# Sums of squares of all norms by products with a column of ones instead of transposes and a reduction

## The chip, the cores and the metric

The program runs on one core of one Trainium2 chip. The metric is the device time of one execution in microseconds. Five engines work side by side, each through its own queue in order: TensorE (PE; its weight loads are listed apart as PEld), VectorE (DVE), ScalarE (ACT), GpSimd (POOL) and SyncE (SP, which issues DMAs). Matmul results land in PSUM, from which VectorE and ScalarE read.

## The reference

The model is a trunk of two layers over 512 tokens of 1024 channels, in float32. Each layer runs three token mixers side by side (differential attention with 4 heads, a convolution module with a depthwise convolution of 31 taps, and neighbourhood attention), merges them by gates, adds the result to the stream, and goes on with a SwiGLU feed-forward and a gated input embedding. Norms stand ahead of each part:

```python
def rmsnorm(x, g):
    x32 = x.astype(jnp.float32)
    y = x32 * lax.rsqrt(jnp.mean(x32 * x32, axis=-1, keepdims=True) + EPS)
    return (y * g.astype(jnp.float32)).astype(x.dtype)
...
for i in range(DEPTH):
    h = rmsnorm(x, norm_mix[i])
    ya = diff_attention(...)       # rmsnorm over 128 channels of each of 4 heads
    yb = conformer_conv(...)       # layernorm over 512 channels
    yc = neighbourhood_attention(...)
    x = x + merged @ w_o[i]
    h = rmsnorm(x, norm_ffn[i])
    x = x + (jax.nn.silu(h @ w_ffn_gate[i]) * (h @ w_ffn_up[i])) @ w_ffn_down[i]
    h = rmsnorm(x, norm_ple[i])
    x = x + jax.nn.sigmoid(h @ w_ple_gate[i]) * (p[i] @ w_ple_in[i])
return rmsnorm(x, norm_final)
```

So 17 means of squares over channels are needed: per layer 3 of the trunk, 4 of the heads and 1 of the convolution, and the final one.

## The kernel before

Activations lie transposed: 128 channels on the partitions, all 512 tokens along the free axis, eight such tiles for 1024 channels. A weight matrix comes in by 128x1024 pieces, and each is split into a high and a low float32r half (ScalarE copies the high half, L143; VectorE subtracts it, L157). A product is then three matmuls of 512 columns (high by high, high by low, low by high, L177 to L179). The feed-forward uses a scheme with 256-column matmuls (L1100).

A norm over channels is a sum across partitions. The squares are first added over the tiles into one 128x512 tile, named `ss` (`sumsq`, or one ScalarE square for a head). Then `norm`, a generator, does the rest. It yields numbers of ticks, so that its parts fall between other matmuls of the stream: TensorE's order is that in which the code issues its instructions, and a tick is four chunks of a product. After the first yield, TensorE transposes `ss` in four 128x128 blocks (L213) into one PSUM bank of the tag `tr`, which has two banks; so the tokens come to the partitions, and the channels' partial sums along the free axis. VectorE adds along that axis (L215) to 128x4 numbers, `sm`: one for each of 512 tokens. A small VectorE operation divides by the number of channels and adds epsilon (L218; for the heads L160, with an epsilon of each token's own). GpSimd raises that to the power -0.5 (L222, `rc`). After the second yield, TensorE turns these columns back into a bank that holds each token's factor on all partitions (L226), ScalarE copies it, and the waiting tiles are multiplied by it.

`main_norm` runs this for the trunk: once in the opening, and in each layer after the output projection (tile `wo_ss`) and after the feed-forward (`ffn_ss`), and once after the first layer's embedding (`ple_ss`). `conv` runs it in each layer, and `diff_unit` once for each head. That is 16 runs. The final norm has code of its own: it takes the sums of six of its eight tiles by four products with a column of ones (L1401), and the rest by VectorE.

Only TensorE's order is fixed by the code. The queues of the other engines are ordered by a scheduler, by priorities and estimated times; so a removed instruction can change the order of others. Pools rotate their buffers: `tr` over two PSUM banks, `sm` over eight small tiles. The names in rows are tiles, with the part of the model in which they were made as a prefix (`diff_tr` is a `tr` bank of the differential attention, `diff_pt` the split transposed probabilities, `pin` and `gateb` projections beside the convolution).

Of the kernel before, what the change touches and what calls it, by code (L numbers as in the profile page):

```python
# [15 lines left out]
ALU = mybir.AluOpType  # L16
AX = mybir.AxisListType
# [3 lines left out]
P = 128  # L21
# [40 lines left out]
class Net:  # L62
# [143 lines left out]
    def norm(self, sq, n, waits, done, spread=True, eps=None):  # L206


        nc = self.nc
        yield waits[0]  # L210
        st = self.ps("tr", (P, 4, P))
        for c in range(4):
            nc.tensor.transpose(st[:, c, :], sq[:, c * P:(c + 1) * P], self.ident)  # L213
        sm = self.sb("sm", [P, 4])
        nc.vector.tensor_reduce(out=sm, in_=st, op=ALU.add, axis=AX.X)  # L215
        ms = self.sb("sm", [P, 4])
        if eps is None:
            nc.vector.tensor_scalar(ms, sm, 1.0 / n, EPS, ALU.mult, ALU.add)  # L218
        else:
            self.stt(ms, sm, 1.0 / n, eps, ALU.mult, ALU.add)  # L220
        col = self.sb("rc", [P, 4])
        nc.gpsimd.tensor_tensor(col, ms, self.power, ALU.pow)  # L222
        yield waits[1]
        bc = self.ps("tr", (P, 4, P))
        for c in range(4):
            nc.tensor.transpose(bc[:, c, :], col[:, c:c + 1].to_broadcast([P, P]), self.ident)  # L226
        bc = bc.rearrange("p a b -> p (a b)")
        done(col, self.spread(bc) if spread else bc)
# [1309 lines left out]
```

## Time and profile before

| | |
|---|---|
| median of 3 runs | 1781.59 us (1780.82 to 1783.68) |
| profiled execution | 1781.65 us |
| its span, first to last instruction | 1779.9 us |
| TensorE matmuls (PE) | 1767.4 us busy, 99% of the span |
| TensorE weight loads (PEld) | 1551.4 us, 87% |
| VectorE (DVE) | 1372.7 us, 77% |
| ScalarE (ACT) | 897.9 us, 50% |
| GpSimd (POOL) | 63.5 us, 4% |
| mean DMA rate | 145 GB/s |

The profile is one execution. In its rows of groups stand line, engine, operation, the tiles (out<-in), the count, and durations in nanoseconds. In rows of the timeline stand start and duration in microseconds, and in brackets the idle time of the engine ahead of that instruction and what ended it. Matmuls are pipelined and overlap, so their durations are longer than the steps between their starts.

### The profile page before, as it was taken

Reading aid. Unit: us, or ns where it says so; the run is one execution under the profiler, and the core shown is the slowest. Engines: PE = TensorE matmul, PEld = TensorE weight load, DVE = VectorE, ACT = ScalarE, POOL = GpSimd, SP = SyncE. Lnnn points to the kernel's source line nnn. Section 1 sums busy time; section 2 is a strip of 40 time slices with the busy share of each in tenths; the row PEclk is TensorE's granted clock in tenths of the full one; section 3 lists DMA queues with packets and bytes.
Section 4 is the critical chain, followed back from the end, with each engine's and each line's share of the span. In section 5 each row is a group of like instructions: output and inputs, shape, how many; then the busy total and the mean of one; then the engine's idle time right before and its main releaser. Section 6 shows DMA issues by size and latency. Waiting matters only on the chain.

```text
span 1779.9 us, 26531 instructions
## 1 busy us (share of the span) xinstructions
PE 1767.4 (99%) x10019; PEld 1551.4 (87%) x10019; DVE 1372.7 (77%) x2113; ACT 897.9 (50%) x1480; POOL 63.5 (4%) x102
## 2 busy tenths in 40 slices
PE   9999999999999999999999999999999999999998
PEld 7888888888899899898878888888888998998987
DVE  7789787897877577577786788879878775775776
ACT  5566555425665255255545664563356652542544
POOL 0000000000010000000000000000000100100000
PEclk9999999999999999999999999999999999999999
DMA  5767443325556366253437564433363662663332
GB/s 190 190 180 189 125 130 93 104 97 163 198 157 180 131 166 189 79 141 115 159 121 189 177 181 119 133 87 107 101 199 133 196 190 84 186 181 107 116 110 95
DMA packets 98384, 257.51 MB, mean 145 GB/s; under 512 B 12880, under 2 KB 17616, under 8 KB 98256
## 3 DMA queue, kind: packets, MB, share of 16 engines
q1 hardware_dynamic: 90912, 231.00, 41.4%
q0 software_dynamic: 6336, 23.07, 7.1%
q8 instruction: 79, 1.29, 0.3%
q10 hardware_dynamic: 1008, 1.75, 0.3%
q14 instruction: 49, 0.40, 0.1%
HBM read 216.44 MB, written 7.86 MB: 126 GB/s over the span
## 4 chain that ended last, share of the span: by engine, by line
PE 96%; DVE 2%; issue 1%; DMA 0%; ACT 0%; SPq 0%; POOL 0%; POOLq 0%; DVEq 0%; ACTq 0%
PE ffn_sc L1100 14%; PE ffn_av L1100 7%; PE ffn_mm L177 4%; PE ffn_mm L178 4%; PE ffn_mm L179 4%; PE ffn_tr L1100 4%; PE mergea_mm L179 2%; PE mergea_mm L177 2%; PE mergea_mm L178 2%; PE wo_mm L178 2%; PE wo_mm L179 2%; PE wo_mm L177 2%; PE gateb_mm L178 2%; PE gateb_mm L179 2%; PE gateb_mm L177 2%; PE natten_mm L177 1%
## 5 line engine op out<-in xcount | busy, mean ns | idle before, releaser
L143 ACT ACTIVATE ffn_wh<-ffn_wr 128x1024 fp32r<-128x1024 f32 (+1 forms) x114 | 117.3, 1029 | 183.2 <-PE ffn_mm L178 102.7
L160 DVE SCALAR_TENSOR_TENSOR conv_z<-glu_z,pre_par,conv_z 128x512 f32<-128x512 f32 x240 | 179.3, 747 | 3.0
L157 DVE TENSOR_TENSOR ffn_wl<-ffn_wr,ffn_wh 128x1024 fp32r<-128x1024 f32 (+1 forms) x114 | 135.0, 1184 | 46.5 <-ACT ffn_wh L143 46.0
L1100 PE MATMUL ffn_sc<-wo_h,ffn_wh 128*128 128x256 f32 x704 | 130.4, 283 | 0.0
L1100 PEld LDWEIGHTS ffn_sc<-wo_h,ffn_wh 128*128 128x128 f32 x704 | 110.4, 192 | 0.8
L1100 PE MATMUL ffn_sc<-wo_h,ffn_wl 128*128 128x256 f32 x352 | 99.6, 283 | 0.0
L177 PE MATMUL ffn_mm<-ffn_z,ffn_wh 128*128 128x512 f32 x240 | 93.4, 389 | 0.0
L178 PE MATMUL ffn_mm<-ffn_z,ffn_wh 128*128 128x512 f32 x240 | 93.4, 389 | 0.0
L179 PE MATMUL ffn_mm<-ffn_z,ffn_wl 128*128 128x512 f32 x240 | 93.4, 389 | 0.0
L157 DVE TENSOR_TENSOR ffn_t<-ffn_mm,wo_r 128x512 f32<-128x512 f32 x48 | 33.1, 689 | 72.3 <-PE ffn_mm L179 72.3
L157 DVE TENSOR_TENSOR ffn_wl<-ffn_rp,ffn_wh 128x1024 fp32r<-128x1024 f32 x44 | 53.8, 1222 | 30.1 <-ACT ffn_wh L143 30.1
L143 ACT ACTIVATE mergea_wh<-mergea_wr 128x1024 fp32r<-128x1024 f32 (+1 forms) x32 | 27.1, 847 | 88.8 <-PE mergea_mm L178 80.4
L1100 PEld LDWEIGHTS ffn_sc<-wo_h,ffn_wl 128*128 128x128 f32 x352 | 67.5, 192 | 0.0
L1100 PE MATMUL ffn_sc<-wo_qk,ffn_wh 128*128 128x256 f32 x352 | 67.1, 283 | 0.0
L1100 PE MATMUL ffn_sc<-wo_v,ffn_wh 128*128 128x256 f32 x352 | 67.1, 283 | 0.0
L1100 PE MATMUL ffn_av<-wo_h,ffn_wh 128*128 128x256 f32 x352 | 65.3, 283 | 0.0
L143 ACT ACTIVATE ffn_wh<-ffn_rp 128x1024 fp32r<-128x1024 f32 x44 | 46.4, 1055 | 29.4 <-PE ffn_mm L178 17.5
L905 DVE TENSOR_REDUCE diff_s<-diff_sc 128x1 f32<-128x512 f32 x64 | 42.7, 685 | 16.1 <-PE diff_sc L808 15.9
L1100 PEld LDWEIGHTS ffn_sc<-wo_qk,ffn_wh 128*128 128x128 f32 x352 | 54.9, 192 | 0.0
L1100 PEld LDWEIGHTS ffn_av<-wo_h,ffn_wh 128*128 128x128 f32 x352 | 54.9, 192 | 0.0
L1100 PEld LDWEIGHTS ffn_sc<-wo_v,ffn_wh 128*128 128x128 f32 x352 | 54.9, 192 | 0.0
L179 PEld LDWEIGHTS ffn_mm<-ffn_z,ffn_wl 128*128 128x128 f32 x240 | 45.1, 188 | 9.4
(726 smaller groups left out, 5635.4 us busy)
## 6 DMA issues: line engine op xcount, KB each, us to landing
ffn_wr<-w_gu SPq DMA_DIRECT2D x66, 512.0 KB, 4.2
ffn_e<-w_gu SPq DMA_DIRECT2D x32, 512.0 KB, 3.4
ffn_e<-w_gu POOLq DMA_DIRECT2D x32, 512.0 KB, 8.0
ffn_wr<-w_fd SPq DMA_DIRECT2D x32, 512.0 KB, 4.7
natten_wr<-w_in SPq DMA_DIRECT2D x16, 512.0 KB, 4.5
natten_b<-bias SPq DMA_DIRECT2D x32, 256.0 KB, 4.3
gatec_wr<-w_in SPq DMA_DIRECT2D x16, 512.0 KB, 4.4
diff_wr<-w_in SPq DMA_DIRECT2D x16, 512.0 KB, 4.7
```

The costliest lines, as they stand in the source:

```text
L143: i = self.nc.scalar.activation(out, in_, func, **kw)
L157: return self.nc.vector.tensor_tensor(out, a, b, op)
L160: return self.nc.vector.scalar_tensor_tensor(out, a, s, b, op0, op1)
L177: mm(out, wh, ah, start=first, stop=False)
L178: mm(out, wh, al, start=False, stop=False)
L179: mm(out, wl, ah, start=False, stop=last)
L905: nc.vector.tensor_reduce(out=m[:, u:u + 1], in_=sc, op=ALU.max, axis=AX.X, negate=True)
L1100: mm(bank[:, u], w[:, u, kp], t, start=begin and n == 0, stop=False, skip_group_check=True)
```

## The change

In `norm`, the four transposes of the squares are replaced by four matmuls: the block of squares is the stationary operand, and one column of ones is the moving one. Each gives a column of 128 sums, one for each token of the block, so the sums come out of TensorE finished, as 128x4 numbers in PSUM. The VectorE reduction is gone, and the small operation reads the sums from PSUM. All 16 runs of `norm` change; the final norm does not. Both operands are float32, as in the final norm's products. From the line after the matmul on, line numbers are one lower than before.

```diff
         nc = self.nc
         yield waits[0]
-        st = self.ps("tr", (P, 4, P))
+        sm = self.ps("tr", (P, 4))
         for c in range(4):
-            nc.tensor.transpose(st[:, c, :], sq[:, c * P:(c + 1) * P], self.ident)
-        sm = self.sb("sm", [P, 4])
-        nc.vector.tensor_reduce(out=sm, in_=st, op=ALU.add, axis=AX.X)
+            nc.tensor.matmul(sm[:, c:c + 1], sq[:, c * P:(c + 1) * P], self.ones[:, 0:1],
+                             start=True, stop=True)
         ms = self.sb("sm", [P, 4])
         if eps is None:
             nc.vector.tensor_scalar(ms, sm, 1.0 / n, EPS, ALU.mult, ALU.add)
```

On TensorE the places stay the same. Around the second layer's convolution norm there stands before:

```order
L179 MATMUL pin_sc_12459<-pin_e_12357,pin_wl_12462 128x512
L213 MATMUL conv_tr_12472<-pre_ident_95,conv_ss_12395 128x128 x4
L177 MATMUL gateb_mm_12486<-ple_h_8751,gateb_wh_12488 128x512
L178 MATMUL gateb_mm_12486<-ple_h_8751,gateb_wh_12488 128x512
L179 MATMUL gateb_mm_12486<-ple_h_8751,gateb_wl_12489 128x512
```

and now:

```order
L179 MATMUL pin_sc_12433<-pin_e_12331,pin_wl_12436 128x512
L213 MATMUL conv_tr_12446<-pre_ones_102,conv_ss_12369 128x1 x4
L177 MATMUL gateb_mm_12458<-ple_h_8733,gateb_wh_12460 128x512
L178 MATMUL gateb_mm_12458<-ple_h_8733,gateb_wh_12460 128x512
L179 MATMUL gateb_mm_12458<-ple_h_8733,gateb_wl_12461 128x512
```

Only the group in the second row is another instruction; the same holds for all 16.

VectorE at that norm, before:

```order
L157 TENSOR_TENSOR pin_wl_12559<-pin_wr_12557,pin_wh_12558 128x256
L215 TENSOR_REDUCE conv_sm_12477<-conv_tr_12472 128x4
L157 TENSOR_TENSOR gateb_wl_12575<-gateb_wr_12573,gateb_wh_12574 128x1024
L218 TENSOR_SCALAR conv_sm_12479<-conv_sm_12477 128x4
L157 TENSOR_TENSOR conv_z_8801<-conv_z_8801,conv_r_12510 128x512
```

and now:

```order
L157 TENSOR_TENSOR pin_wl_12531<-pin_wr_12529,pin_wh_12530 128x256
L217 TENSOR_SCALAR conv_sm_12451<-conv_tr_12446 128x4
L157 TENSOR_TENSOR gateb_wl_12547<-gateb_wr_12545,gateb_wh_12546 128x1024
L157 TENSOR_TENSOR conv_z_8783<-conv_z_8783,conv_r_12482 128x512
L157 TENSOR_TENSOR conv_z_9753<-conv_z_9753,conv_r_12482 128x512
```

The reduction is gone, and the small operation on `conv_sm` now stands ahead of the weight split `gateb_wl` instead of behind it.

VectorE behind the norm of the first head (first layer), where the probabilities of the next head are made (`diff_s`, `diff_a`) and transposed (`diff_pt`), before:

```order
L905 TENSOR_REDUCE diff_s_2474<-diff_sc_2475 128x1
L157 TENSOR_TENSOR diff_rp_2393<-diff_rp_2393,diff_kh_2253 128x512
L905 TENSOR_REDUCE diff_s_2474<-diff_sc_2481 128x1
L160 SCALAR_TENSOR_TENSOR conv_z_1492<-glu_z_318,pre_par_67,conv_z_1492 128x512
L157 TENSOR_TENSOR diff_pt_2519<-diff_tr_2514,diff_pt_2519 128x512
L910 RECIPROCAL diff_s_2474<-diff_s_2474 128x1
L160 SCALAR_TENSOR_TENSOR conv_z_1492<-glu_z_318,pre_par_67,conv_z_1492 128x512
L160 SCALAR_TENSOR_TENSOR diff_s_2474<-diff_s_2474,natten_nlam_540,diff_sm_2000 128x1
L157 TENSOR_TENSOR diff_pt_2527<-diff_tr_2522,diff_pt_2527 128x512
L157 TENSOR_TENSOR gatec_wl_2736<-gatec_wr_2734,gatec_wh_2735 128x1024
L160 SCALAR_TENSOR_TENSOR diff_a_2479<-diff_e_2485,diff_s_2474,diff_a_2479 128x512
```

and now:

```order
L904 TENSOR_REDUCE diff_s_2470<-diff_sc_2471 128x1
L904 TENSOR_REDUCE diff_s_2470<-diff_sc_2477 128x1
L157 TENSOR_TENSOR diff_rp_2391<-diff_rp_2391,diff_kh_2251 128x512
L160 SCALAR_TENSOR_TENSOR conv_z_1490<-glu_z_316,pre_par_67,conv_z_1490 128x512
L909 RECIPROCAL diff_s_2470<-diff_s_2470 128x1
L157 TENSOR_TENSOR diff_pt_2515<-diff_tr_2510,diff_pt_2515 128x512
L160 SCALAR_TENSOR_TENSOR diff_s_2470<-diff_s_2470,natten_nlam_538,diff_sm_1998 128x1
L160 SCALAR_TENSOR_TENSOR conv_z_1490<-glu_z_316,pre_par_67,conv_z_1490 128x512
L160 SCALAR_TENSOR_TENSOR diff_a_2475<-diff_e_2481,diff_s_2470,diff_a_2475 128x512
L157 TENSOR_TENSOR gatec_wl_2732<-gatec_wr_2730,gatec_wh_2731 128x1024
L157 TENSOR_TENSOR diff_pt_2523<-diff_tr_2518,diff_pt_2523 128x512
```

The second `diff_pt` moved from ahead of `gatec_wl` and `diff_a` to behind them, and the first from ahead of the reciprocal to behind it. ScalarE's queue shows the matching move there: the second copy to `diff_pt` now stands behind the second exponential (`diff_e`). Behind the second head's norm the second `diff_pt` moves too, behind `diff_a` alone, while the first stays ahead of the reciprocal. In the second layer the moves are the same.

## The prediction

> **What bounds the kernel now.** I read the page first: busy shares, granted clock, chain of work.
>
> ```profile
> span 1779.9 us, 26531 instructions
> ...
> PE 1767.4 (99%) x10019; PEld 1551.4 (87%) x10019; DVE 1372.7 (77%) x2113; ACT 897.9 (50%) x1480; POOL 63.5 (4%) x102
> ...
> PEclk9999999999999999999999999999999999999999
> ...
> PE 96%; DVE 2%; issue 1%; DMA 0%; ACT 0%; SPq 0%; POOL 0%; POOLq 0%; DVEq 0%; ACTq 0%
> ```
>
> TensorE is busy for 99% of the span at full clock, and 96% of the chain that ended last is its own work, with VectorE at 2%. Since the ends of matmuls are modelled, I take no busy time as a price. I go by steps, from the start of one matmul to the start of the next, and by the table of what TensorE waited for:
>
> ```profile
> PE diff_av L177 <- DVE diff_v L157: 2.8, 2, 1.4
> ...
> PE ple_tr L213 <- DVE ple_ss L157: 1.0, 1, 1.0
> PE natten_mm L598 <- DVE natten_t L160: 0.8, 1, 0.8
> ...
> PE conv_tr L226 <- POOL conv_rc L222: 0.4, 1, 0.4
> ```
>
> These waits come to 5.0 us in 1780. The first three are for the split of the values, for a sum of squares not yet added, and for a projection; in none is the norm's VectorE reduction the last thing. Only the fourth lies behind a norm's sums. So what the change adds to TensorE's stream should be paid nearly in full, and what it takes from VectorE should return only where TensorE stands behind a norm.
>
> **How often.** The edited lines run once per norm. The transposes they remove, by tile:
>
> ```profile
> L213 PE MATMUL diff_tr<-pre_ident,diff_ss x32: 270/272/273, 236.9 to 1204.8; 128*128 128x128 f32 x32
> ...
> L213 PE MATMUL conv_tr<-pre_ident,conv_ss x8: 271/272/273, 414.2 to 1296.0; 128*128 128x128 f32 x8
> ...
> L213 PE MATMUL wo_tr<-pre_ident,wo_ss x8: 272/272/273, 502.5 to 1382.2; 128*128 128x128 f32 x8
> ...
> L213 PE MATMUL ffn_tr<-pre_ident,ffn_ss x8: 270/272/273, 850.0 to 1729.7; 128*128 128x128 f32 x8
> ...
> L213 PE MATMUL glu_tr<-pre_ident,glu_ss x4: 271/272/273, 27.9 to 28.2; 128*128 128x128 f32 x4
> ...
> L213 PE MATMUL ple_tr<-pre_ident,ple_ss x4: 272/272/303, 895.6 to 896.0; 128*128 128x128 f32 x4
> ```
>
> That is 64 transposes, four to a norm: 16 norms (8 of attention heads, 2 of the convolution, 6 of the trunk). The seventeenth, at the kernel's end, doesn't use this code.
>
> **Removed from TensorE: four transposes.** The timeline of TensorE around the first head's norm:
>
> ```profile
> 236.68 0.39 PE L179 MATMUL gateb_mm<-glu_h,gateb_wl 128*128 128x512 f32 x1
> 236.91 0.60 PE L213 MATMUL diff_tr<-pre_ident,diff_ss 128*128 128x128 f32 x4
> 237.26 0.48 PE L808 MATMUL diff_sc<-diff_qk 128*128 128x512 f32 x1
> 237.58 0.40 PE L808 MATMUL diff_sc<-diff_x,diff_qk 128*128 128x512 f32 x1
> ```
>
> The four start at 236.91 and the next matmul at 237.26: 0.35 us. That next one takes 0.32 us instead of the 0.23 of the step before the group; its weights could not be loaded under a long matmul. I expect this 0.09 us after the new products too, which are as short, so it drops out.
>
> **Added to TensorE: four products with one column.** This very form stands in the kernel's last stage, where the last norm gets most of its sums so:
>
> ```profile
> 1761.28 0.60 PE L1344 MATMUL ple_av<-pre_ident,ple_h 128*128 128x128 f32 x4
> 1761.63 0.36 PE L1337 MATMUL ple_mm<-ple_wh,ffn_v 128*128 128x256 f32 x1
> ...
> 1762.31 0.28 PE L1339 MATMUL ple_mm<-ple_wh,ffn_v 128*128 128x256 f32 x1
> 1762.43 0.95 PE L1401 MATMUL ple_mm<-pre_ones,ple_ss 128*128 128x1 f32 x8
> 1763.24 0.41 PE L1344 MATMUL ple_tr<-pre_ident,ple_h 128*128 128x128 f32 x2
> ```
>
> ```profile
> L1401 PE MATMUL ple_mm<-pre_ones,ple_ss x8: 166/250/250, 1762.4 to 1763.1; 128*128 128x1 f32 x8
> ```
>
> Four products in the code are eight matmuls in the trace: a product of two float32 operands goes through the array twice, each pass with its own load of 128x128 weights, while a transpose goes once. From 1762.43 to the next start at 1763.24 it is 0.81 us; four transposes nearby take 1761.63 - 1761.28 = 0.35 us, as above. One column instead of 128 saves nothing, since the pass lasts as long as its load, about 0.10 us. So a norm costs 0.81 - 0.35 = 0.46 us more on TensorE, and 16 norms 7.4 us. Its lower end is 0, if the second pass vanished under the neighbours; its upper end is 0.46 + 0.09 = 0.55 us a norm (8.8 in all), if the load after the group were less covered than now. I take 0.46: same form, same operands' types.
>
> [...]
>
> **Removed from VectorE: the sum along rows.**
>
> ```profile
> L215 DVE TENSOR_REDUCE diff_sm<-diff_tr x8: 682/684/686, 240.0 to 1205.9; 128x4 f32<-128x512 f32 x8
> ...
> L215 DVE TENSOR_REDUCE ffn_sm<-ffn_tr x2: 692/692/692, 850.6 to 1730.0; 128x4 f32<-128x512 f32 x2
> ...
> L1404 DVE TENSOR_SCALAR ple_sm<-ple_mm x1: 163/163/163, 1763.4 to 1763.4; 128x4 f32<-128x4 f32 x1
> ```
>
> Sixteen of 0.684 to 0.692 us are 11.0 us of VectorE. The small operation behind them now reads PSUM; L1404 does just that in 0.163 us, so it costs nothing more. VectorE is 77% busy and TensorE seldom waits for it, so I book the 11.0 us at zero, except where TensorE stands behind them. There are two such places.
>
> The first is the second layer's convolution norm:
>
> ```profile
> 1296.29 0.69 DVE L215 TENSOR_REDUCE conv_sm<-conv_tr 128x4 f32<-128x512 f32 x1 [1.10 <-PE conv_tr L213]
> 1296.90 1.22 DVE L157 TENSOR_TENSOR gateb_wl<-gateb_wr,gateb_wh 128x1024 fp32r<-128x1024 f32 x1
> 1298.03 0.16 DVE L218 TENSOR_SCALAR conv_sm<-conv_sm 128x4 f32<-128x4 f32 x1
> ```
>
> ```profile
> 1298.37 1.01 POOL L222 TENSOR_TENSOR conv_rc<-conv_sm,pre_power 128x4 f32<-128x4 f32 x1 [89.62 <-DVE conv_sm L218]
> ```
>
> ```profile
> 1298.61 0.39 PE L179 MATMUL gateb_mm<-ple_h,gateb_wl 128*128 128x512 f32 x1
> 1299.43 0.65 PE L226 MATMUL conv_tr<-pre_ident,conv_rc 128*128 128x128 f32 x4 [0.43 <-POOL conv_rc L222]
> ```
>
> From 1298.61 to 1299.43 is 0.82 us where a step is 0.23: a stall of 0.59 us. A weight split of 1.22 us stands between the reduction and the small operation; in the new order nothing does. The small operation starts 0.98 us after the products (1763.41 - 1762.43 at the end of the kernel), GpSimd's power is then done about 1.3 us before TensorE arrives, and the 0.59 us goes (at least 0, at most 0.59).
>
> The second is a transpose that waited for a PSUM bank which a reduction still read:
>
> ```profile
> PEld diff_tr L862 <- DVE diff_sm L215: 0.3, 1, 0.3
> ```
>
> The small operation frees the bank some 0.5 us sooner, and TensorE comes 0.46 us later: 0.3 us goes.
>
> **What moves.** TensorE's order stands but for the substituted group. VectorE's and ScalarE's queues change their order in both layers behind the first two head norms. ScalarE now does the second exponential ahead of the second copy of transposed probabilities, and VectorE finishes that copy's remainder (diff_pt) after a weight split and a combination of probabilities instead of before (at the second head, after the combination alone). What waits for it on TensorE is the product with the values:
>
> ```profile
> 245.33 0.69 DVE L157 TENSOR_TENSOR diff_pt<-diff_tr,diff_pt 128x512 fp32r<-128x512 f32 x1
> 245.93 1.22 DVE L157 TENSOR_TENSOR gatec_wl<-gatec_wr,gatec_wh 128x1024 fp32r<-128x1024 f32 x1
> 247.06 0.75 DVE L160 SCALAR_TENSOR_TENSOR diff_a<-diff_e,diff_s,diff_a 128x512 f32<-128x512 f32 x1
> ...
> 248.82 0.28 PE L177 MATMUL diff_av<-diff_pt,diff_v 128*128 128x256 f32 x1
> ```
>
> It ends at 246.02 and the product starts at 248.82: 2.8 us of room, against 1.22 + 0.75 = 1.97 us put ahead of it and 0.69 taken out. I book 0 at all four places. No DMA moves.
>
> **The sum.** 7.4 - 0.6 - 0.3 = +6.5 us. The profiled execution took 1781.65 us (the span and 1.75 us around it); the median of the runs is 1781.59, the same. So 1788.1 us, 0.36% slower. From no change a measurement of this kernel can tell about 0.2%, 3.6 us: the forecast lies outside.
>
> **Rivals.**
>
> Same: the extra passes vanish in TensorE's slack. The load column is busy 87% of the span, not 99%, so 228 us would be open to loads, and eight loads for four might fit under the 512-column neighbours. Then the 7.4 us goes, the 0.9 us of credits stays, and the time is 1780.8. Against it: at 1762.43 the next matmul did wait 0.81 us. [...] Chance 9%.
>
> Faster: VectorE is what really holds TensorE back, through lateness that the wait table spreads over other names. The place is the mixer stages, where diff_av and natten_mm wait. Price: 11.0 us returned against 7.4 added is -3.6, 1778.0 us. It decides only if nearly 11 us of TensorE's idle time ends, and there are 1779.9 - 1767.4 = 12.5 us of it in all; the four listed waits, 5.0 us, would leave +2.1. Chance 3%.
>
> [...] Chance 2%.
>
> Slower by a new wait: the diff_pt remainder comes late at the four places. Without its cover it could cost 1.97 us at each first head and 0.75 at each second, 5.4 more: 1793.5 us. It decides once more than 2.8 us are put ahead of it. Chance 3%.
>
> **How the numbers follow.** The forecast holds 83%. Its low end takes the two waits for diff_v (2.8 us) as gone too: 1785.3. Its high end takes the products at their upper price, 8.8, and drops both credits: 1790.4. The range 1785.2 to 1790.5 leaves out the rivals, 17%. Slower 83 + 2 + 3 = 88%, same 9%, faster 3%.
>
> **What would show it.** After: 128 short matmuls at the norms' line, each group holding TensorE for about 0.81 us; no reduction on VectorE there, its busy time down by 11; no wait of conv_tr for GpSimd. Wrong, if the groups hold TensorE for 0.4 us, or if TensorE's waits fall by more than 4 us or grow by more than 2.

## The result

The changed kernel takes 1789.75 us in the median (1788.45 to 1790.43), the kernel before 1781.59: a ratio of 1.0044, with a 95% interval of 1.0031 to 1.0057. It is slower by 8.2 us; the forecast was 6.5 us slower. The profiled execution took 1790.43 us, 1.73 us more than its span of 1788.7 us, and the span has grown by 8.8 us.

The page of the profile after, shares and chain:

```profile
span 1788.7 us, 26635 instructions
...
PE 1775.4 (99%) x10083; PEld 1559.6 (87%) x10083; DVE 1362.8 (76%) x2097; ACT 899.0 (50%) x1480; POOL 67.5 (4%) x102
...
PE 86%; DVE 2%; DMA 2%; ACT 0%; SPq 0%; issue 0%; POOLq 0%; POOL 0%; DVEq 0%; ACTq 0%
```

TensorE has 64 more instructions (10083 against 10019) and is busy 8.0 us longer. VectorE has 16 fewer and is busy 9.9 us less, and the kernel is slower all the same. The products' line of the profile after, first and last tile:

```profile
L213 PE MATMUL diff_tr<-pre_ones,diff_ss x64: 164/250/250, 238.1 to 1212.3; 128*128 128x1 f32 x64
...
L213 PE MATMUL ple_tr<-pre_ones,ple_ss x8: 242/250/250, 900.0 to 900.7; 128*128 128x1 f32 x8
```

There are 128 matmul records for 64 products, eight to a norm; a record is called a pass below. TensorE's timeline of the profile after, at the first head's norm:

```profile
237.90 0.39 PE L179 MATMUL gateb_mm<-glu_h,gateb_wl 128*128 128x512 f32 x1
238.13 0.95 PE L213 MATMUL diff_tr<-pre_ones,diff_ss 128*128 128x1 f32 x8
238.94 0.49 PE L807 MATMUL diff_sc<-diff_qk 128*128 128x512 f32 x1
239.26 0.40 PE L807 MATMUL diff_sc<-diff_x,diff_qk 128*128 128x512 f32 x1
```

The group holds the stream from 238.13 to 238.94, 0.81 us, and the matmul behind it takes 0.32 us (238.94 to 239.26), as it did behind the transposes. Over the 16 norms, from the first short matmul to the start of the next long one, the groups take 13.00 us; before they took 5.70 us. The difference is 7.3 us, 0.46 a norm. What TensorE waited for, after:

```profile
PE diff_av L177 <- DVE diff_v L157: 2.8, 2, 1.4
...
PE ple_tr L213 <- DVE ple_ss L157: 1.0, 1, 1.0
PE diff_av L597 <- DVE natten_y L157: 0.8, 1, 0.8
PE natten_mm L597 <- DVE natten_t L160: 0.8, 1, 0.8
```

The wait of conv_tr for GpSimd is gone from the list, and the wait for natten_y is new. The second layer's convolution norm after, on VectorE, GpSimd and TensorE:

```profile
1304.25 0.16 DVE L217 TENSOR_SCALAR conv_sm<-conv_tr 128x4 f32<-128x4 f32 x1 [1.45 <-PE conv_tr L213]
1304.38 1.23 DVE L157 TENSOR_TENSOR gateb_wl<-gateb_wr,gateb_wh 128x1024 fp32r<-128x1024 f32 x1
```

```profile
1304.56 1.91 POOL L221 TENSOR_TENSOR conv_rc<-conv_sm,pre_power 128x4 f32<-128x4 f32 x1 [89.87 <-DVE conv_sm L217]
```

```profile
1306.71 0.39 PE L179 MATMUL gateb_mm<-ple_h,gateb_wl 128*128 128x512 f32 x1
1306.94 0.60 PE L225 MATMUL conv_tr<-pre_ident,conv_rc 128*128 128x128 f32 x4
```

The weight split now stands behind the small operation, and TensorE goes on after a step of 0.23 us (1306.71 to 1306.94): the stall of 0.59 us has ended. GpSimd's operation spanned 1.91 us here and 1.01 before, so it ended 0.47 us ahead of TensorE (1304.56 + 1.91 against 1306.94).

**Where 8.8 us of span went.** Followed matmul by matmul, the starts on TensorE fall behind those of before by 7.3 us in the 16 groups. They gain 0.6 us at the convolution, 0.2 us at the PSUM bank, 0.2 us at the transposes L225 of the first head in the second layer, and 0.3 us in the first 7 us, where the steps of 512 columns shrink from 0.43 to 0.23 us earlier than before. Three losses belong to no step of the forecast: 1.0 us at 200 us, which is the new wait for natten_y, 1.55 us between 902 and 906 us, and 0.3 us at a product of the feed-forward at 1477 us. 7.3 - 0.6 - 0.2 - 0.2 - 0.3 + 1.0 + 1.55 + 0.3 = 8.85; smaller shifts make up the difference from 8.8.

The 1.55 us lie behind the norm `ple`, where no engine is waited for. TensorE's timeline after:

```profile
899.97 1.02 PE L213 MATMUL ple_tr<-pre_ones,ple_ss 128*128 128x1 f32 x8 [0.96 <-DVE ple_ss L157]
900.85 0.49 PE L177 MATMUL glu_mm<-ple_pt,glu_wh 128*128 128x512 f32 x1
...
902.74 0.63 PE L178 MATMUL glu_mm<-ple_pt,glu_wh 128*128 128x512 f32 x1
903.17 0.63 PE L179 MATMUL glu_mm<-ple_pt,glu_wl 128*128 128x512 f32 x1
```

From 902.74 to 903.17 is 0.43 us for a 512-wide step that takes 0.23 elsewhere. The same place by stretches, after (the last columns are the granted clock, the share of the DMA engines and GB/s):

```profile
902.00:903.00 1.00, 1.00 (x5) 0.81 (x4) 0.00 (x0) 0.69 (x1) 0.45 (x2) 0.68 0.00 0
903.00:904.00 1.00, 1.00 (x3) 0.73 (x3) 0.61 (x1) 0.36 (x1) 0.00 (x0) 0.50 0.00 0
904.00:905.00 1.00, 1.00 (x4) 0.78 (x3) 0.62 (x1) 0.26 (x1) 0.00 (x0) 0.50 0.00 0
905.00:910.00 5.00, 5.00 (x24) 4.05 (x23) 1.90 (x3) 1.39 (x2) 0.00 (x0) 0.92 0.70 206
```

The granted clock is 0.5 for 0.64 + 1 + 1 + 0.8 = 3.4 us, and 1.0 on either side. The page's row of clocks, a digit for each 45 us, reads 9 throughout and doesn't show it. In the profile before no such stretch follows this norm. There the four transposes stand from 895.6 to 896.0 us, and behind them the steps stay at 0.23 us. One of the stretches before:

```profile
898.00:899.00 1.00, 1.00 (x6) 0.82 (x5) 0.46 (x1) 0.63 (x2) 0.44 (x2) 1.00 0.00 0
```

### The profile page after: what moved, and what is told of

The parts are those of the page before. It is cut to its first block, busy times and chain, and to the rows that moved or that the text cites. A ratio compares the mean times of both kernels' runs of the same rounds, so it can differ in the third digit from the quotient of the medians.

```text
span 1788.7 us, 26635 instructions
## 1 busy us (share of the span) xinstructions
PE 1775.4 (99%) x10083; PEld 1559.6 (87%) x10083; DVE 1362.8 (76%) x2097; ACT 899.0 (50%) x1480; POOL 67.5 (4%) x102
## 3 DMA queue, kind: packets, MB, share of 16 engines
HBM read 216.44 MB, written 7.86 MB: 125 GB/s over the span
## 4 chain that ended last, share of the span: by engine, by line
PE 86%; DVE 2%; DMA 2%; ACT 0%; SPq 0%; issue 0%; POOLq 0%; POOL 0%; DVEq 0%; ACTq 0%
PE ffn_sc L1099 14%; PE ffn_av L1099 7%; PE ffn_mm L178 4%; PE ffn_mm L179 4%; PE ffn_mm L177 4%; PE ffn_tr L1099 4%; PE mergea_mm L179 2%; PE mergea_mm L177 2%; PE mergea_mm L178 2%; PE gateb_mm L177 2%; PE gateb_mm L178 2%; PE gateb_mm L179 2%; PE wo_mm L177 2%; PE wo_mm L178 2%; PE wo_mm L179 2%; PE diff_sc L807 1%
```

## Experiments

My theory after the result had two parts. The steady part is the forecast's: each norm costs TensorE 0.46 us, and what VectorE saves is worth nothing but the two stalls. The new part (Theory A): the low clock follows from TensorE's wait and the one-column products together, at the one norm where TensorE waits for its squares. The rivals: some of the 7.3 us is paid by VectorE after all; the clock falls by chance, whatever the kernel (Rival B); the fall comes from the wait alone.

### The same kernel again

> The changed kernel once more, nothing edited. In its first profile the granted clock fell to 0.5 from 902.35 to 905.76 us, right behind the norm of the embedding (ple_ss), and nine 512-wide steps there took 0.43 us instead of 0.23, which cost 1.55 us; a stall of 0.98 us at the first product of the last block of values (199.7 us) stood behind a rotation's DMA. [...] The stall at 199.7 should not be there, if it was a late DMA.

1790.44 us against 1781.79, a ratio of 1.0046 (1.0033 to 1.0059). The groups take 13.00 us again, and the clock falls again behind the same norm. Of the stretches of this profile:

```profile
901.00:902.00 1.00, 1.00 (x4) 0.71 (x4) 0.03 (x1) 0.00 (x0) 0.82 (x1) 0.50 0.00 0
```

With 0.94 in the stretch ahead of this one, 0.50 in the two behind it and 0.86 in the next, it lasts from 900.88 to 904.28 us, 3.4 us. The late start at 200 us, which I had expected to be absent, is there too: 0.67 us of TensorE's steps.

### Products added to the kernel before, nothing taken away

```diff
         for c in range(4):
+            nc.tensor.matmul(st[:, c, 0:1], sq[:, c * P:(c + 1) * P], self.ones[:, 0:1],
+                             start=True, stop=True)
+        for c in range(4):
             nc.tensor.transpose(st[:, c, :], sq[:, c * P:(c + 1) * P], self.ident)
```

> Before, with the four products issued in addition, into columns that the transposes then overwrite: the price of the products by itself. By steps: 16 x 0.81 = 13.0 us more, 1794.6, or 1796.2 with a low clock behind the ple norm. Rival (the loads are covered by the 512-wide neighbours): under 3 us more, below 1784.6.

1794.97 us against 1781.79: 13.2 us more, a ratio of 1.0074 (1.0061 to 1.0088). 16 x 0.81 is 13.0. So the price of the products holds where VectorE still does all of its reductions, and it does not vanish under the neighbours. TensorE's timeline and the stretches of this run at the norm `ple`:

```profile
902.18 1.02 PE L213 MATMUL ple_tr<-pre_ones,ple_ss 128*128 128x1 f32 x8 [0.97 <-DVE ple_ss L157]
903.06 0.63 PE L216 MATMUL ple_tr<-pre_ident,ple_ss 128*128 128x128 f32 x4
903.45 0.48 PE L177 MATMUL glu_mm<-ple_pt,glu_wh 128*128 128x512 f32 x1
```

```profile
904.00:906.00 2.00, 2.00 (x10) 1.65 (x9) 0.61 (x3) 1.06 (x1) 1.11 (x2) 1.00 0.00 0
```

The same wait and the same products stand here, and the clock stays at 1.0 in the profiled execution (1794.44 us). This speaks against the new part as I had put it. The four executions took 1794.34, 1794.44, 1795.51 and 1795.71 us; whether the longer two had a fall isn't known, so this stays open (below).

### The reduction taken away, the transposes kept

```diff
-        sm = self.sb("sm", [P, 4])
-        nc.vector.tensor_reduce(out=sm, in_=st, op=ALU.add, axis=AX.X)
+        sm = st[:, :, 0]
```

> Before, without VectorE's reduction and nothing in its place: the small operation reads one of the 128 transposed columns of each block, so the factors of the 16 norms are wrong numbers, and TensorE's four transposes stay. It prices the 11.0 us taken from VectorE. Forecast's view: only the two stalls behind norms go, 0.6 + 0.3: 1780.9. Rival (VectorE's lateness holds TensorE back): up to 11.0 us less, 1770.8.

This kernel leaves the sum out: the small operation reads one transposed column of each block. 1783.23 us against 1781.76, a ratio of 1.0008 (0.9999 to 1.0017). VectorE is 10.6 us less busy, nothing is added to TensorE, and no time came back. The stalls at the convolution and at the bank are gone from the trace, but there is a new one. VectorE and TensorE at the second head of the second layer, in this run:

```profile
1156.34 0.16 DVE L909 RECIPROCAL diff_s<-diff_s 128x1 f32<-128x1 f32 x1 [0.32 <-ACT diff_e L143]
...
1156.80 0.75 DVE L160 SCALAR_TENSOR_TENSOR diff_a<-diff_e,diff_s,diff_a 128x512 f32<-128x512 f32 x1
1157.46 1.28 DVE L157 TENSOR_TENSOR diff_pt<-diff_tr,diff_pt 128x512 fp32r<-128x512 f32 x2
```

```profile
1158.30 0.62 PE L225 MATMUL diff_tr<-pre_ident,diff_rc 128*128 128x128 f32 x4 [1.22 <-DVE diff_pt L157]
```

and in the profile after:

```profile
1161.74 0.69 DVE L157 TENSOR_TENSOR diff_pt<-diff_tr,diff_pt 128x512 fp32r<-128x512 f32 x1 [0.50 <-ACT diff_pt L143]
1163.08 0.16 DVE L909 RECIPROCAL diff_s<-diff_s 128x1 f32<-128x1 f32 x1 [0.65 <-ACT diff_e L143]
```

```profile
1164.02 0.60 PE L225 MATMUL diff_tr<-pre_ident,diff_rc 128*128 128x128 f32 x4
```

Here both remainders diff_pt stand behind the reciprocal and the combination of probabilities, and TensorE waits 1.2 us for the first of them, which frees the PSUM bank for the transposes of L225. In the changed kernel only the second remainder has moved there; the first stays ahead of the reciprocal, and TensorE does not wait. So this stall belongs to the order that VectorE has in this run, and it hides part of what the missing reduction returns. The run shows that nothing near 11 us returns. What does return is told better by the run with one pass (below), whose VectorE has the changed kernel's order at this place.

### The norm `ple` alone: transposes there, or products only there

```diff
+        if self.phase == "ple":
+            st = self.ps("tr", (P, 4, P))
...
+            nc.vector.tensor_reduce(out=sm, in_=st, op=ALU.add, axis=AX.X)
+        else:
             sm = self.ps("tr", (P, 4))
...
```

> The change at 15 norms; the one of the embedding (ple_ss) keeps transposes and reduction. Theory A: no low clock at 900 us, and 0.46 + 1.55 = 2.0 us less than the changed kernel: 1787.7. Rival B: the low clock stays (or comes as chance has it) and only 0.46 us goes: 1789.3.

> Before, with the change at the one norm of the embedding alone. Theory A: low clock for 3.4 us behind it, 0.46 + 1.55 = 2.0 us more than before: 1783.6. Rival B: 0.46 us more, 1782.1.

With transposes at `ple` and products at the other 15 norms: 1788.18 us against 1781.79, 6.4 more, a ratio of 1.0040 (1.0027 to 1.0052). The clock stays at 1.0 behind the norm, though TensorE waits there as before. Of its stretches:

```profile
900.00:903.00 3.00, 3.00 (x15) 2.43 (x14) 1.57 (x3) 1.41 (x2) 1.11 (x2) 1.00 0.00 0
```

The median is 1.6 to 2.3 us below the changed kernel's two, of which 0.46 is the one norm's products. (The profiled execution of this run was longer than its median, 1791.65 us, by waits of the feed-forward for ffn_y.)

With products at `ple` alone (the condition turned round): 1782.80 us (1780.57 to 1784.17), a ratio of 1.0004 (0.9995 to 1.0013). One norm's 0.46 and a fall's 1.55 would be 2.0 us; the times can't tell 0.5 from 2.0. The profile can: in it the clock falls at 897.60 us (0.80 in the stretch from 897 to 898) and stays low to 901 us at least.

```profile
898.00:899.00 1.00, 1.00 (x4) 0.81 (x3) 0.00 (x0) 0.00 (x0) 1.00 (x2) 0.50 0.00 0
```

So the fall needs nothing of the change at the other 15 norms. But it does not come in every execution. The mean granted clock over the span is known for each of the eleven, in thousandths: two have 1.000, and a stretch of 3.41 us at 0.5 would take 0.001 from it. Three have 0.998; apart from the run with 40 products more (below), only the changed kernel shows values as low. Chance has a part in it, then, as Rival B had it, though not the whole.

This run also bears on the late start at 200 us, since up to 895 us its program is that of the kernel before. VectorE in the profile after and in this run:

```profile
197.13 0.69 DVE L157 TENSOR_TENSOR diff_rp<-diff_rp,diff_r 128x512 f32<-128x512 f32 x1 [1.08 <-DMA diff_rp<-diff_rp]
```

```profile
196.89 0.69 DVE L157 TENSOR_TENSOR diff_rp<-diff_rp,diff_r 128x512 f32<-128x512 f32 x1 [0.90 <-DMA diff_rp<-diff_rp]
```

VectorE waits for a small DMA that landed 3.7 us after its issue in the profile after, 3.4 us in this run, and 2.0 us in the profile before; everything behind it on VectorE is late, natten_y too. So the delay can come with nothing of the change ahead of it. That does not clear the change: a wait stands here in four profiles with two-pass products at the norms ahead of it (VectorE's for the DMA of 1.08 us after and 0.77 us when the kernel ran again; TensorE's for natten_y of 0.3 us with products added and 0.6 us with the sums one tick later), and in two without such products the DMA landed after 2.2 us (no reduction) and 2.0 us (one pass). TensorE lost 0.3 to 1.0 us by it. Whether the products make the delay likelier isn't settled.

### No wait at `ple`: the sums taken one tick later

```diff
-        self.main_norm(st[0], (3, 2), x=x)
+        self.main_norm(st[0], (4, 1), x=x)
```

> The changed kernel with the sums of the embedding's norm issued one tick (12 matmuls of 512 columns) later and its second half at the old place, so that ple_ss is there when TensorE comes. The wait of 1.1 us before them goes (-1.1), and with it, if the low clock needs wait and short products together, the low clock (up to -1.55): 1787.1 to 1788.7. Rival (the short products alone cause it): low clock still there in the profile, 1789.3. If the second half then waits for GpSimd's power, part of the 1.1 us stays.

> Before, with the same shift of the embedding's norm and no other edit. The wait of 1.1 us goes, and there was no low clock to lose: 1780.7.

The changed kernel with this edit: 1788.27 us, a ratio of 1.0038 (1.0025 to 1.0051). TensorE in its trace:

```profile
900.04 0.50 PE L178 MATMUL glu_mm<-ple_b,glu_wh 128*128 128x512 f32 x1 [0.29 <-DVE ple_b L160]
...
902.01 0.95 PE L213 MATMUL ple_tr<-pre_ones,ple_ss 128*128 128x1 f32 x8
902.82 0.48 PE L177 MATMUL glu_mm<-ple_y,glu_wh 128*128 128x512 f32 x1
```

The products wait for nothing, all 16 groups are there, and the clock stays at 1.0. But the wait itself was not saved: about 1 us of it comes back as waits for ple_b ahead of the norm. So the 1.5 us below the changed kernel's 1789.75 are about what one fall costs.

The kernel before with this edit: 1782.23 us, a ratio of 1.0002 (0.9993 to 1.0010), where I had expected 1780.7. A miss: the wait for ple_ss turned into waits for ple_b (1.0 us in TensorE's steps) and for the norm's own factors. Of this run's waits:

```profile
PE ple_tr L226 <- POOL ple_rc L222: 0.5, 1, 0.5
...
PE glu_mm L178 <- DVE ple_b L160: 0.3, 1, 0.3
```

VectorE is as late as before; TensorE's new order only changes at which instruction the wait shows.

### Many one-column products, many transposes

In the kernel before, ahead of the transposes of the first layer's `wo` norm:

```diff
+        if self.phase == "wo" and self.i == 0:
+            for c in [0, 1, 2, 3] * 10:
+                nc.tensor.matmul(st[:, c, 0:1], sq[:, c * P:(c + 1) * P], self.ones[:, 0:1],
+                                 start=True, stop=True)
```

The other run has `* 18` and a transpose in the loop.

> Before, with 40 more one-column products in a row (results overwritten) at the norm behind the first layer's output projection, in the middle of a dense stream of matmuls. Price by steps: 80 passes x 0.10 = 8.1 us. Theory A (one-column products look idle to whatever sets the clock): the granted clock falls to 0.5 within about two windows of 3.41 us after they begin at 502 us. Rival C (only a TensorE that waits does): the clock stays 1.0 there. With A one window at half clock adds up to 1.7 us behind or in it.

> The same place with 72 more transposes instead of products: 72 x 0.11 = 7.9 us. Theory A, if it is the columns that count: a transpose moves 128 columns in 0.11 us, about half of what the array could, and the clock stays 1.0. If transposes look idle too, the clock falls as with the products, and the difference between the two at the embedding's norm is only that the products take 0.5 us longer.

With the products 1797.71 us against 1782.22, a ratio of 1.0089 (1.0060 to 1.0119); with the transposes 1788.63, 6.4 us more, a ratio of 1.0038 (1.0022 to 1.0054), which the expected 7.9 us fits. The products, timeline and stretches:

```profile
502.60 14.60 PE L214 MATMUL wo_tr<-pre_ones,wo_ss 128*128 128x1 f32 x80
```

```profile
502.00:505.00 3.00, 3.00 (x30) 3.00 (x28) 1.29 (x2) 0.00 (x0) 0.89 (x1) 1.00 0.17 22
505.00:508.00 3.00, 3.00 (x18) 3.00 (x17) 0.00 (x0) 0.00 (x0) 0.00 (x0) 0.55 0.82 153
508.00:511.00 3.00, 3.00 (x16) 3.00 (x15) 0.00 (x0) 0.00 (x0) 0.00 (x0) 0.50 0.02 5
...
520.00:525.00 5.00, 5.00 (x29) 4.72 (x28) 3.31 (x4) 3.68 (x5) 0.28 (x1) 0.76 0.00 0
```

The products cost 15.5 us, where I had expected 8.1 and up to 1.7 for one stretch of 3.41 us at half clock. TensorE and its loads are busy without a gap, and 2.7 us after the first product the clock goes to 0.5 and stays there for 17.1 us by the stretches, five times 3.41. The passes then take about 0.19 us (16 in 3 us) instead of 0.10. The transposes, timeline and stretches:

```profile
501.97 8.02 PE L214 MATMUL wo_tr<-pre_ident,wo_ss 128*128 128x128 f32 x72
```

```profile
505.00:508.00 3.00, 3.00 (x30) 3.00 (x29) 0.00 (x0) 0.00 (x0) 0.00 (x0) 1.00 0.59 117
508.00:511.00 3.00, 3.00 (x30) 3.00 (x29) 0.53 (x1) 0.00 (x0) 0.00 (x0) 1.00 0.00 0
```

The transposes load the same kind of 128x128 tile as often (30 in 3 us), and the clock stays at 1.0. So the 80 passes of one-column products in a row did not hold the clock up, and the 72 transposes did. Whether it is the single column or the two passes, no run tells apart.

### One pass instead of two

The squares are held as float32r, and the products take two columns of float32r ones; the sums are read from the first column of each pair. What this changes in the computation: the added squares are rounded to float32r.

```diff
-            st.append(self.sb("ss", [P, 512]))
+            st.append(self.sb("ss", [P, 512], F32R))
...
-        sm = self.ps("tr", (P, 4))
+        st = self.ps("tr", (P, 4, 2))
+        sm = st[:, :, 0]
         for c in range(4):
-            nc.tensor.matmul(sm[:, c:c + 1], sq[:, c * P:(c + 1) * P], self.ones[:, 0:1],
+            nc.tensor.matmul(st[:, c, :], sq[:, c * P:(c + 1) * P], self.ones_r[:, 0:2],
...
```

> The change with sums of squares kept as float32r and two float32r columns of ones, so that each product goes through the array once. If the price of the change is the second pass, four products take about what four transposes take (4 x 0.10 to 0.11 us), and the 0.9 us of stalls that went stay gone: 1780.9 to 1781.8, with a low clock behind the ple norm less likely, since the group is as short as the transposes. Rival (the price is that of the product's form, one or two columns, whatever the passes): 1788 to 1790 as in the changed kernel.

> The one-pass version once more, against before on another chip or at another time. Its group took 0.36 us in the first profile, as four transposes do (0.35), and 0.5 us of stall behind the convolution norm and 0.2 at a PSUM bank were gone: 0.5 to 1.0 us less than before, about 1781. Rival: no difference from before.

1780.84 us against 1781.76, a ratio of 0.9995 (0.9986 to 1.0004), and again 1781.14 against 1781.69, 0.9997 (0.9988 to 1.0006). TensorE at the first head's norm in this run:

```profile
236.24 0.39 PE L179 MATMUL gateb_mm<-glu_h,gateb_wl 128*128 128x512 f32 x1
236.46 0.50 PE L214 MATMUL diff_tr<-pre_onesr,diff_ss 128*128 128x2 f32 x4
236.83 0.49 PE L808 MATMUL diff_sc<-diff_qk 128*128 128x512 f32 x1
```

Four passes hold the stream for 0.37 us, about as four transposes did; over the 16 norms 5.88 us against 5.70. The clock stays at 1.0. This version is about 9 us faster than the changed kernel and can't be told from the kernel before: the intervals hold 1, with 0.6 to 0.9 us less in both medians. VectorE is 10.5 us less busy here too. On TensorE the stalls at the convolution (0.6 us) and at the bank (0.2 us) are gone and no new wait has come, so what the reduction's time returns is these stalls and little else.

## Why the prediction was right, and where it was too small

**The products' price: right.** 16 x 0.46 = 7.4 us was said, 7.3 measured. It was paid in full: the run with products alone added cost 13.2 us for 16 x 0.81 = 13.0, and no rival in which the passes vanish fits that. The load column at 87% was no slack. No run shows a product of more than two passes, to which the forecast gave 2%: the trace has 128 records for 64 products. The run with one pass shows that the second pass is what the change costs: 0.37 us a norm with four passes, 0.81 with eight.

**The reduction at zero: right.** VectorE is 9.9 us less busy in the changed kernel, and the kernel is slower. The run with one pass takes the reductions away at nearly no price on TensorE and gets back 0.6 to 0.9 us, and the run without the reduction, with 1.2 us of a new wait of its own, was no faster. That ends the rival by VectorE's lateness, which needed 11.

**The two stalls: right.** 0.59 and 0.3 us were said, 0.6 and 0.2 measured. My reason for the first was too generous in its margin: I had GpSimd done 1.3 us ahead of TensorE, and it was 0.47, because GpSimd's operation spanned 1.91 us and not 1.01.

**The moved remainders at zero: right in the profile after, for a thin reason.** I looked for the harm at the product with the values, where there was 2.8 us of room. The place that was near its limit is the PSUM bank that the first remainder frees for L225. In the profile after it cost nothing. When the same kernel ran again, L225 waited 0.3 us at the first head of the second layer, where the first remainder now stands behind the reciprocal; it started 0.15 us after that remainder's end, as it did in the run without the reduction. In the run without the reduction, whose first remainder moved further at the second head, it cost 1.2 us.

**The clock: the step that failed.** The first part of the prediction read the clock as full throughout and priced every step at it. The sum of +6.5 us is close to what the kernels do whose profiles show no fall: 6.4 us with products at 15 norms (15 x 0.46 - 0.9 = 6.0 by the forecast's terms), 6.5 us with the wait moved away (1788.27 - 1781.76). The agreement is in part luck, since their profiles also hold 0.3 and 0.75 us of the loss at 200 us. The changed kernel has 8.2 to 8.7 us, and nine steps of 0.43 instead of 0.23 us are 1.55 us by the traces' steps: 6.5 + 1.55 = 8.05. The forecast has no term for the 1.0 us at 200 us either. The median stayed inside the range, but not by any term that I had put there: its high end stood for dearer products and kept stalls.

**What is shown of the cause, and what isn't.** Shown: the clock falls to 0.5 behind `ple` in all three profiles of kernels that have the change at this norm with its wait (at 902.35, 900.88 and 897.60 us), though not in every execution (two of the eleven with products at `ple` alone have a mean clock of 1.000); it stays at 1.0 in the profiles with transposes there, with one pass there, or with the wait moved; 80 one-column passes without a gap brought the clock down by themselves, 72 transposes didn't. The fall of the profile after lasts 3.413 us and begins 263 times 3.413 us after the clock first rises there (at 4.64 us, where the 512-wide steps shrink); in the profile before the clock rises at 6.92 us and next falls at 1778.44 us, behind the last matmul, 519 times 3.413 us later. Worked out from the traces, by steps: in the 3.41 us ahead of its fall in the profile after TensorE had waited or done one-column products for 1.9 us; in the profile before, waiting and transposes at this norm came to 1.5 us. Not shown: why the fall comes in some executions alone. No profile shows the changed kernel without the fall, and each profile that lacks it is one execution, so a comparison with it alone is weak. Nor did the wait and the products always suffice: the profile with products and transposes at every norm has 2.0 us of waiting and one-column products at `ple`, without a break, and the clock stays at 1.0. What more it takes isn't settled. Nor do the runs tell why the DMA at 200 us lands late in some executions.

## What to carry to other kernels

Price work added to TensorE by the steps between starts and count its passes: here a float32 product took two, a transpose or a float32r product one, and narrow results saved nothing (0.10 us a pass with one column, 0.09 us with the 128 of a transpose). Taking work from an engine with slack gave back only the stalls that could be named (here 0.6 to 0.9 us for 10.5 us of VectorE), and it moved the engine's queue, so look for the buffer that the moved instruction frees, not only for its reader. Behind short products and a wait of TensorE the granted clock fell to 0.5 for some 3.4 us in three profiles here, which the profile's coarse row of clocks hides; look at a microsecond's stretches there.

## What was unexpected of the hardware

- Matmuls with one result column did not hold the clock up: with 80 passes in a row, PE and loads busy throughout, the granted clock fell to 0.5 after 2.7 us and stayed there for 17.1 us; passes went from 0.10 to 0.19 us.
- 72 transposes in 7.86 us, 0.109 us each, kept the clock at 1.0.
- One fall, 3.41 us at half clock, cost 1.55 us where TensorE's stream was full.
- The same small DMA landed 2.0 us after its issue in the profile before and 3.4 us in that with products at `ple` alone, with nothing changed ahead of it; in the profile after it took 3.7 us, and TensorE lost 1.0 us by it.
